# Attention products of two tensor-engine halves tied together, half 1 issued ahead of half 0

## The chip, the cores and the metric

The kernel runs on one core of a Trainium2 chip. Its engines work in parallel, each through its own queue and in that queue's order: TensorE (PE) multiplies matrices into PSUM banks, VectorE (DVE) and ScalarE (ACT) do the elementwise work and read PSUM, and SyncE (SP) issues the transfers from HBM. They wait for each other by semaphores. The metric is the time of one execution in microseconds (us), lower being better; a single core has one time per run.

## The reference

A first transformer block is followed by a network of two layers, over 256 tokens of width 1024, in float32. What matters here are its attention parts.

- The first block's mixer adds three things side by side: a gated linear attention (GLA, 4 heads), a causal convolution, and a differential attention with 4 heads, in which each head has two softmax maps over 64-wide halves of its queries and keys: `a = softmax(q1 k1^T) - lam * softmax(q2 k2^T)`, then `a v`. Group-routed experts follow.
- Each layer has a feed-forward block, a mixer and a second feed-forward block, all scaled by vectors that a large matrix `w_ada` gives from a condition `c` (`c_act @ w_ada`). The mixer adds a sparse attention with 8 heads (compressed, selected and window branches), a "forgetting" attention (FOX, 4 heads) whose scores get `F[q] - F[k]` added, and a block attention (MOBA, 4 heads). With 256 tokens, FOX and MOBA are plain causal softmax attentions with heads of width 64:

```
s = q k^T / 8   (+ F[q] - F[k] for FOX);  p = softmax(where(k <= q, s, -inf));  o = p v
```

## The kernel before

**Tiling.** Activations are kept with features on the 128 partitions. Weights come by DMA into `raw` tiles of 1 MB, ACT rounds them to a reduced float32 (`hi`, line 313), DVE computes the rest (`lo`, line 317), and PE multiplies with both. Most PE time is in these weight products (lines 334 to 355, 604, and the experts).

**Attention.** A head is 64 wide, half of PE's 128 rows or columns. In the scores (line 939 for the differential attention, line 1492 for FOX and MOBA in `causal`) the head of half 0 has its queries and keys on partitions 0 to 63, the head of half 1 on 64 to 127; each uses 64 of PE's rows. One set of scores has eight products: two halves, two heads `e`, and two query blocks, the first with 128 keys and the second with 256. The halves write different PSUM tiles: `pse` (half 0) and `psd` (half 1) in the differential attention, `psa` and `pse` in `causal`. Then come, on PE, the mask (`mask_pair`, lines 970 and 971; for FOX also the products with `NB`, line 1499), the row maxima on DVE (`neg_max`, 977 and 978), the exponentials on ACT (`act`, 487), scaling on DVE (957 and 958, or 1518 and 1519), transposes on PE (`prob_t`, 985 to 987, copied by 384 or 386), and the products with the values: 961 and 962 with full width, 1524 in `causal`, where each half uses 64 of PE's columns. These are in plain float32, and each such matmul is two records of the trace.

**The conditioning.** The products with `w_ada` (line 1060, tiles `araw` into `psm`) are spread over the whole program as a side job: `ada_step` takes one 1 MB tile, four matmuls that each use 32 of PE's columns (two per step in the last block of a layer). In the mixers the tiles come from a pool of two buffers, so the load of one waits until the matmuls of the one two before it are done.

**What sets the order.** The Python loops only give the dependencies and the program order. A list scheduler places the instructions of each engine by its own estimate of when each is ready; PSUM and SBUF pools with one or two buffers (rings `a`, `d`, `e` of two banks each, `n` and `m` of one) limit what is open. On the chip each engine then runs its list strictly in order. So in one engine's list the parts are mixed: weight products, conditioning and attention alternate. `after` (line 491) can add an ordering dependency without a semaphore between two instructions; before the change only the activation tables and the splits in `split` use it.

Of the kernel before, what the change touches and what calls it, by code (L numbers as in the profile page):

```python
# [20 lines left out]
P = 128  # L21
# [203 lines left out]
class Net:  # L225
# [266 lines left out]
    def after(self, ins, prev):  # L492
        self.tc.add_manual_dep(ins.ins, prev.ins.name, mybir.DependencyInfo(
            mybir.DependencyClass.NoSync, mybir.DependencyReason.DATA), reason="activation table")

    def table(self, name):
        ins = self.tc.keep_in_program_order(self.nc.scalar.preload_act_table_set(name))
        if self.tab is not None and self.tab[0] is self.nc.cur_bb:
            for p in [self.tab[1]] + self.tab[2]:
                self.after(ins, p)  # L500
        self.tab = (self.nc.cur_bb, ins, [])
# [308 lines left out]
    def gla(self, T, lr, gw, qk, gv, sog):  # L810


        nc = self.nc
        qT, kT = qk
# [5 lines left out]
        g = T([P, 256], "gg")  # L820
        self.log_sigmoid(g, L, 256, T)
        EX = T([P, 8, 256], "gEX")
        for t in range(2):
            for b in range(2):
                pe = self.ps("a")
                o = (t + 4 * b) * P
# [49 lines left out]
        for p in range(2):  # L876
            po = self.ps("a")

            for t, S_, o, q, st, sp in ((0, SA, 0, 0, True, True), (0, SX, 0, P, True, False), (1, SA, 4, P, False, True)):
                for e in range(2):  # L880
                    h = 2 * p + e
                    nc.tensor.matmul(po[64 * e:64 * e + 64, q:q + P], gv[:, t, 64 * h:64 * h + 64], S_[:, o + h, :], start=st,
                                     stop=sp, tile_position=(0, 64 * e))
            nc.scalar.activation(sq[:, 256 * p:256 * p + 256], po[:, 0:256], AF.Square)
            nc.vector.tensor_tensor(go[:, p, :], po[:, 0:256], sog[p], OP.mult)
        return go, sq

    def diff1(self, T, ss, nat, dv):
        nc = self.nc
# [5 lines left out]
        for i in range(2):  # L895
            for t in range(2):
                o = (2 * i + t) * 8
# [32 lines left out]
        for hp in range(2):  # L930
            pw = {}

            pms = [[self.ps(ring), self.ps(ring)] for ring in "ed"]
            for e in range(2):
                h = 2 * hp + e
                for i, (q, n) in enumerate(((0, P), (P, 256))):
                    for m in range(2):
                        r = slice(64 * m, 64 * m + 64)
                        nc.tensor.matmul(pms[m][i][:, e * n:e * n + n], qT[r, h, q:q + P], kT[r, h, 0:n], start=(e == 0),
                                         stop=False, skip_group_check=True)  # L940
            for m in range(2):
                p0, p1 = pms[m]
                self.mask_pair(p0, p1)
# [475 lines left out]
    def selected(self, T, kT, vn, qT, sg, po):  # L1419
# [3 lines left out]
        for rp in range(2):  # L1423
# [37 lines left out]
            for b in range(2):  # L1461
                for i in range(4):
                    for t, w in ((0, P0[i]), (1, P1[i])):
                        nc.vector.tensor_scalar(w[:, b], w[:, b], su[:, t, i // 2, i % 2, b:b + 1], None, OP.mult)

                for t, kt in ((0, 0), (1, 0), (1, 1)):
                    pt = self.ps("a")
                    for i in range(4):
                        src = P0[i][:, b] if t == 0 else P1[i][:, b, kt * P:(kt + 1) * P]
                        nc.tensor.transpose(pt[:, i * P:(i + 1) * P], src, ident)  # L1470
                    pT = T([P, 512], "apT", 3)
                    self.cp(pT, pt)
                    for g in range(2):
                        v0 = P * (1 + b) + 64 * g
                        nc.tensor.matmul(po[t][64 * g:64 * g + 64, 256 * rp:256 * rp + 256], vn[:, kt, v0:v0 + 64],  # L1475
                                         pT[:, 256 * g:256 * g + 256], start=False, stop=(b == 1 and kt == t and rp == 1),
                                         tile_position=(0, 64 * g), skip_group_check=True)

    def causal(self, T, mix, c0, qT, kT, ko, v, vo, NB):

# [3 lines left out]
        su = T([P, 4, 2], "su2", 2)  # L1484
        w0s = T([P, 2, 2, P], "aP0", 3)

        pms = [[self.ps(ring), self.ps(ring)] for ring in "ae"]
        for e in range(2):
            for i, (q, n) in enumerate(((0, P), (P, 256))):
                for hb in range(2):  # L1490
                    r = slice(64 * hb, 64 * hb + 64)
                    nc.tensor.matmul(pms[hb][i][:, e * n:e * n + n], qT[r, e, q:q + P], kT[r, ko + e, 0:n], start=(e == 0),
                                     stop=False, skip_group_check=True)
        for hb in range(2):
            p0, p1 = pms[hb]
            if NB is not None:
# [15 lines left out]
        for e in range(2):  # L1512
            po = self.ps("n")
            pTs = []
            for hb in range(2):
                h = 2 * e + hb
                w0, w1 = pw[h]
                nc.vector.tensor_scalar(w0, w0, su[:, h, 0:1], None, OP.mult)
                nc.vector.tensor_scalar(w1, w1, su[:, h, 1:2], None, OP.mult)
                pTs.append(self.prob_t(w0, w1))  # L1520
            for t in range(2):
                for hb in range(2):
                    o = vo + 64 * (2 * e + hb)
                    nc.tensor.matmul(po[64 * hb:64 * hb + 64, t * P:256], v[:, t, o:o + 64], pTs[hb][:, 256 * t:256 + P * t],
                                     start=(t == 0), stop=(t == 1), tile_position=(0, 64 * hb))
            self.put_hl(mix, c0 + e, po[:, 0:256])

    def final(self):
# [412 lines left out]
```

## Time and profile before

| | |
|---|---|
| Median of 3 runs | 1452.15 us (1451.53 to 1452.27) |
| Profiled execution | 1456.9 us, its span 1455.1 us |
| PE busy | 1411.1 us, 97% of the span |
| DVE busy | 1138.2 us, 78% |
| ACT busy | 856.0 us, 59% |
| HBM read | 324.13 MB, 223 GB/s over the span |

The places of the change are: the first mixer with line 939 (83 to 100 us) and the GLA products (116 to 118 us), the selected branch with line 1475 (from 633 us in layer 0, to 1207 us in layer 1), FOX and MOBA with lines 1492 and 1524 (671 to 699 us in layer 0, 1217 to 1243 us in layer 1). A matmul's busy time in the trace includes its way through the array, so that the records of consecutive matmuls overlap; what one costs is read from the start of the next.

### The profile page before, as it was taken

How to read it: one execution, taken by the hardware profiler on the slowest of the kernel's cores; microseconds unless marked ns; L12 is line 12 of the kernel's file. 1: busy time of each engine (PE TensorE's matmuls, PEld its weight loads, DVE VectorE, ACT ScalarE, POOL GpSimd, SP SyncE). 2: the span in 40 equal slices, each digit the busy share in tenths (PEclk: the TensorE clock that was granted, in tenths of full speed). 3: DMA queues.
4: the chain of work that ended last, by engine and by line, in shares of the span. 5: the costliest groups of instructions: out<-in, count | busy, mean ns of one | idle time of the engine just before them, and what ended most of it. 6: DMA issues, size and time to landing. Idle time of an engine off the chain costs nothing.

```text
span 1455.1 us, 22278 instructions
## 1 busy us (share of the span) xinstructions
PE 1411.1 (97%) x8093; PEld 1145.8 (79%) x8093; DVE 1138.2 (78%) x2557; ACT 856.0 (59%) x1575; POOL 0.2 (0%) x4
## 2 busy tenths in 40 slices
PE   7999699999999999999999999999999999999997
PEld 6755478778888888676788889888888677888886
DVE  8996478888999667485899886998687586887664
ACT  7545277777756555364755555666555464766553
POOL 0000000000000000000000000000000000000000
PEclk9999889999999999999999999999999999999999
DMA  8734557887887557543388686787477552275452
GB/s 306 276 129 165 236 202 261 298 324 275 326 318 271 198 184 266 194 169 116 136 294 309 226 297 214 284 315 261 159 263 290 211 194 87 90 241 191 158 179 69
DMA packets 51396, 326.67 MB, mean 224 GB/s; under 512 B 6209, under 2 KB 7378, under 8 KB 18898
## 3 DMA queue, kind: packets, MB, share of 16 engines
q1 hardware_dynamic: 50994, 325.00, 61.6%
q8 instruction: 65, 1.06, 0.3%
q14 instruction: 49, 0.40, 0.1%
q10 hardware_dynamic: 288, 0.20, 0.1%
HBM read 324.13 MB, written 1.05 MB: 223 GB/s over the span
## 4 chain that ended last, share of the span: by engine, by line
PE 79%; DVE 2%; ACT 2%; DMA 1%; issue 0%; DVEq 0%; ACTq 0%; SPq 0%
PE psd L337 12%; PE psa L337 11%; PE pse L337 10%; PE psd L339 7%; PE psa L339 6%; PE pse L339 5%; PE psd L353 2%; PE psm L1060 2%; PE psd L354 2%; PE psd L355 2%; PE psd L1732 1%; PE psd L1733 1%; PE psd L1731 1%; PE pse L1475 1%; PE pse L1754 1%; DVE lo L317 1%
## 5 line engine op out<-in xcount | busy, mean ns | idle before, releaser
L317 DVE TENSOR_TENSOR lo<-raw,hi 128x512 fp32r<-128x512 f32 x992 | 605.1, 639 | 164.9 <-ACT hi L313 162.6
L313 ACT ACTIVATE hi<-raw 128x1024 fp32r<-128x1024 f32 (+3 forms) x498 | 485.1, 980 | 347.7 <-PE psd L337 80.7
L337 PE MATMUL psd<-hl,hi 128*128 128x512 f32 x624 | 225.0, 402 | 7.8 <-ACT hi L313 7.0
L339 PE MATMUL psd<-hl,lo 128*128 128x256 f32 x656 | 185.0, 284 | 0.0
L337 PE MATMUL psa<-hl,hi 128*128 128x512 f32 x464 | 165.2, 397 | 1.2 <-ACT hi L313 1.2
L337 PE MATMUL pse<-hl,hi 128*128 128x512 f32 x464 | 164.3, 396 | 0.0
L337 PEld LDWEIGHTS psd<-hl,hi 128*128 128x128 f32 x624 | 117.9, 190 | 40.1 <-ACT hi L313 8.5
L339 PE MATMUL pse<-hl,lo 128*128 128x256 f32 x512 | 143.0, 280 | 0.0
L339 PE MATMUL psa<-hl,lo 128*128 128x256 f32 x496 | 138.7, 281 | 0.0
L339 PEld LDWEIGHTS psd<-hl,lo 128*128 128x128 f32 x656 | 124.7, 190 | 1.9 <-DVE lo L317 0.9
L337 PEld LDWEIGHTS psa<-hl,hi 128*128 128x128 f32 x464 | 87.2, 188 | 22.6 <-ACT hi L313 1.9
L337 PEld LDWEIGHTS pse<-hl,hi 128*128 128x128 f32 x464 | 87.3, 188 | 20.8 <-ACT w L384 0.3
L339 PEld LDWEIGHTS pse<-hl,lo 128*128 128x128 f32 x512 | 96.5, 189 | 0.2
L339 PEld LDWEIGHTS psa<-hl,lo 128*128 128x128 f32 x496 | 93.6, 189 | 0.8 <-DVE lo L317 0.4
L1089 DVE SCALAR_TENSOR_TENSOR acc<-araw,cact,acc 128x512 f32<-128x512 f32 x118 | 85.8, 748 | 1.6 <-DMA araw<-wada 1.6
L353 PE MATMUL psd<-hi,hl 128*128 128x512 f32 (+3 forms) x224 | 84.4, 377 | 0.8 <-ACT hl L375 0.4
L354 PE MATMUL psd<-lo,hl 128*128 128x512 f32 (+3 forms) x224 | 83.6, 373 | 0.0
L355 PE MATMUL psd<-hi,hl 128*128 128x512 f32 (+3 forms) x224 | 83.3, 374 | 0.0
L337 PE MATMUL psd<-hT,hi 128*128 128x512 f32 x220 | 77.6, 395 | 0.0
L337 PE MATMUL psa<-hT,hi 128*128 128x512 f32 x220 | 77.4, 394 | 0.0
L339 PE MATMUL psd<-hT,lo 128*128 128x256 f32 x264 | 74.2, 281 | 0.0
L339 PE MATMUL psa<-hT,lo 128*128 128x256 f32 x264 | 74.1, 281 | 0.0
(564 smaller groups left out, 2605.2 us busy)
## 6 DMA issues: line engine op xcount, KB each, us to landing
raw<-w SPq DMA_DIRECT2D x88, 1024.0 KB, 4.9
araw<-wada SPq DMA_DIRECT2D x64, 1024.0 KB, 6.7
raw<-w SPq DMA_DIRECT2D x64, 704.0 KB, 4.2
raw<-egu SPq DMA_DIRECT2D x32, 1024.0 KB, 5.0
raw<-edn SPq DMA_DIRECT2D x16, 1024.0 KB, 4.9
raw<-w2n SPq DMA_DIRECT2D x12, 1024.0 KB, 6.5
raw<-cw SPq DMA_DIRECT2D x8, 1024.0 KB, 5.8
araw<-wadb SPq DMA_DIRECT2D x8, 1024.0 KB, 5.7
```

The lines of the kernel that those rows point to most:

```text
L313: nc.scalar.activation(hi[:, f:g], src[:, f:g], AF.Copy)
L317: ins = nc.vector.tensor_tensor(lo[:, f:g], src[:, f:g], hi[:, f:g].bitcast(F32), OP.subtract)
L337: nc.tensor.matmul(ps[:M, :].rearrange("p (a b) -> p a b", a=2), hi[:, o:o + M], xhl[:, k0 + k, :, :], start=st, stop=False)
L339: nc.tensor.matmul(ps[:M, 0:256], lo[:, o:o + M], xhl[:, k0 + k, 0, :], start=False, stop=sp)
L353: nc.tensor.matmul(o, xh, wh, start=st, stop=False)
L354: nc.tensor.matmul(o, xh, wl, start=False, stop=False)
L355: nc.tensor.matmul(o, xl, wh, start=False, stop=sp)
L1060: self.nc.tensor.matmul(self.ada_acc[32 * j:32 * j + 32, :], lhsT, rhs[:, 512 * j:512 * j + 512], start=start, stop=stop, tile_position=(0 ...
L1089: nc.vector.scalar_tensor_tensor(acc[:, w], raw[:, w], self.cact[:, c, 0:1], acc[:, w], OP.mult, OP.add)
L1475: nc.tensor.matmul(po[t][64 * g:64 * g + 64, 256 * rp:256 * rp + 256], vn[:, kt, v0:v0 + 64], pT[:, 256 * g:256 * g + 256], start=False, s ...
L1731: nc.tensor.matmul(pg, xh(c), wh, start=(c == 0), stop=False)
L1732: nc.tensor.matmul(pg, xh(c), wl, start=False, stop=False)
```

## The change

A new helper `halves` issues the product of half 1, then that of half 0, and adds an ordering dependency between them, so that half 0 can't stand ahead of half 1 on PE. Where `prev` is given (the two score functions), the first product of a pair also follows the second product of the pair before, so that the eight products of a set keep one order. The dependency orders a pair; other instructions may still stand between. It is used in five places: GLA's values, the scores of the differential attention, the selected branch's values, and scores and values of `causal`. No product is added or removed.

```diff
--- before.py
+++ after.py
@@ -493,6 +493,15 @@
         self.tc.add_manual_dep(ins.ins, prev.ins.name, mybir.DependencyInfo(
             mybir.DependencyClass.NoSync, mybir.DependencyReason.DATA), reason="activation table")
 
+    def halves(self, product, prev=None):
+
+
+        first, second = (product(h) for h in (1, 0))
+        self.after(second, first)
+        if prev is not None:
+            self.after(first, prev)
+        return second
+
     def table(self, name):
         ins = self.tc.keep_in_program_order(self.nc.scalar.preload_act_table_set(name))
         if self.tab is not None and self.tab[0] is self.nc.cur_bb:
@@ -877,10 +886,9 @@
             po = self.ps("a")
 
             for t, S_, o, q, st, sp in ((0, SA, 0, 0, True, True), (0, SX, 0, P, True, False), (1, SA, 4, P, False, True)):
-                for e in range(2):
-                    h = 2 * p + e
-                    nc.tensor.matmul(po[64 * e:64 * e + 64, q:q + P], gv[:, t, 64 * h:64 * h + 64], S_[:, o + h, :], start=st,
-                                     stop=sp, tile_position=(0, 64 * e))
+                self.halves(lambda e: nc.tensor.matmul(
+                    po[64 * e:64 * e + 64, q:q + P], gv[:, t, 128 * p + 64 * e:128 * p + 64 * e + 64], S_[:, o + 2 * p + e, :],
+                    start=st, stop=sp, tile_position=(0, 64 * e)))
             nc.scalar.activation(sq[:, 256 * p:256 * p + 256], po[:, 0:256], AF.Square)
             nc.vector.tensor_tensor(go[:, p, :], po[:, 0:256], sog[p], OP.mult)
         return go, sq
@@ -930,14 +938,13 @@
         for hp in range(2):
             pw = {}
 
-            pms = [[self.ps(ring), self.ps(ring)] for ring in "ed"]
+            pms, pr = [[self.ps(ring), self.ps(ring)] for ring in "ed"], None
             for e in range(2):
                 h = 2 * hp + e
                 for i, (q, n) in enumerate(((0, P), (P, 256))):
-                    for m in range(2):
-                        r = slice(64 * m, 64 * m + 64)
-                        nc.tensor.matmul(pms[m][i][:, e * n:e * n + n], qT[r, h, q:q + P], kT[r, h, 0:n], start=(e == 0),
-                                         stop=False, skip_group_check=True)
+                    pr = self.halves(lambda m: nc.tensor.matmul(
+                        pms[m][i][:, e * n:e * n + n], qT[64 * m:64 * m + 64, h, q:q + P], kT[64 * m:64 * m + 64, h, 0:n],
+                        start=(e == 0), stop=False, skip_group_check=True), pr)
             for m in range(2):
                 p0, p1 = pms[m]
                 self.mask_pair(p0, p1)
@@ -1470,11 +1477,10 @@
                         nc.tensor.transpose(pt[:, i * P:(i + 1) * P], src, ident)
                     pT = T([P, 512], "apT", 3)
                     self.cp(pT, pt)
-                    for g in range(2):
-                        v0 = P * (1 + b) + 64 * g
-                        nc.tensor.matmul(po[t][64 * g:64 * g + 64, 256 * rp:256 * rp + 256], vn[:, kt, v0:v0 + 64],
-                                         pT[:, 256 * g:256 * g + 256], start=False, stop=(b == 1 and kt == t and rp == 1),
-                                         tile_position=(0, 64 * g), skip_group_check=True)
+                    self.halves(lambda g: nc.tensor.matmul(
+                        po[t][64 * g:64 * g + 64, 256 * rp:256 * rp + 256], vn[:, kt, P * (1 + b) + 64 * g:P * (1 + b) + 64 * g + 64],
+                        pT[:, 256 * g:256 * g + 256], start=False, stop=(b == 1 and kt == t and rp == 1),
+                        tile_position=(0, 64 * g), skip_group_check=True))
 
     def causal(self, T, mix, c0, qT, kT, ko, v, vo, NB):
 
@@ -1484,13 +1490,12 @@
         su = T([P, 4, 2], "su2", 2)
         w0s = T([P, 2, 2, P], "aP0", 3)
 
-        pms = [[self.ps(ring), self.ps(ring)] for ring in "ae"]
+        pms, pr = [[self.ps(ring), self.ps(ring)] for ring in "ae"], None
         for e in range(2):
             for i, (q, n) in enumerate(((0, P), (P, 256))):
-                for hb in range(2):
-                    r = slice(64 * hb, 64 * hb + 64)
-                    nc.tensor.matmul(pms[hb][i][:, e * n:e * n + n], qT[r, e, q:q + P], kT[r, ko + e, 0:n], start=(e == 0),
-                                     stop=False, skip_group_check=True)
+                pr = self.halves(lambda hb: nc.tensor.matmul(
+                    pms[hb][i][:, e * n:e * n + n], qT[64 * hb:64 * hb + 64, e, q:q + P], kT[64 * hb:64 * hb + 64, ko + e, 0:n],
+                    start=(e == 0), stop=False, skip_group_check=True), pr)
         for hb in range(2):
             p0, p1 = pms[hb]
             if NB is not None:
@@ -1519,10 +1524,9 @@
                 nc.vector.tensor_scalar(w1, w1, su[:, h, 1:2], None, OP.mult)
                 pTs.append(self.prob_t(w0, w1))
             for t in range(2):
-                for hb in range(2):
-                    o = vo + 64 * (2 * e + hb)
-                    nc.tensor.matmul(po[64 * hb:64 * hb + 64, t * P:256], v[:, t, o:o + 64], pTs[hb][:, 256 * t:256 + P * t],
-                                     start=(t == 0), stop=(t == 1), tile_position=(0, 64 * hb))
+                self.halves(lambda hb: nc.tensor.matmul(
+                    po[64 * hb:64 * hb + 64, t * P:256], v[:, t, vo + 64 * (2 * e + hb):vo + 64 * (2 * e + hb) + 64],
+                    pTs[hb][:, 256 * t:256 + P * t], start=(t == 0), stop=(t == 1), tile_position=(0, 64 * hb)))
             self.put_hl(mix, c0 + e, po[:, 0:256])
 
     def final(self):
```

The scheduler then places much else anew. On PE, in the first mixer (the second set of scores is `psd_938`, `psd_939` for half 1 and `pse_936`, `pse_937` for half 0; `araw_1253` to `araw_1271` are successive conditioning tiles; line 961 is line 968 after the change, 1060 is 1067), before:

```order
L1060 MATMUL psm_1248<-araw_1253,cact_363 32x512 x3
L1060 MATMUL psm_1248<-araw_1259,cact_363 32x512 x4
L863 MATMUL psa_1068<-hl_1040,gzk_1065 128x256 x2
L939 MATMUL psd_938<-dT_139_833,dT_136_818 128x128 x2
L970 LDWEIGHTS k_identb
L970 MATMUL psd_938<-k_maskb,k_identb 128x256
L939 MATMUL psd_939<-dT_139_833,dT_136_818 128x256 x2
L985 MATMUL pse_908<-blob,dP_158_880 128x128
L986 MATMUL pse_908<-blob,dP_159_881 128x128
L987 MATMUL pse_908<-blob,dP_159_881 128x128
```

and with the change, from the same place:

```order
L1067 MATMUL psm_1248<-araw_1259,cact_363 32x512 x3
L1067 MATMUL psm_1248<-araw_1265,cact_363 32x512 x4
L872 MATMUL psa_1068<-hl_1040,gzk_1065 128x256 x2
L945 MATMUL psd_938<-dT_139_833,dT_136_818 128x128
L992 MATMUL pse_908<-blob,dP_158_880 128x128
L993 MATMUL pse_908<-blob,dP_159_881 128x128
L994 MATMUL pse_908<-blob,dP_159_881 128x128
L1067 MATMUL psm_1248<-araw_1271,cact_363 32x512
L968 MATMUL pse_914<-w_169_912,ddv_795 128x256
L969 MATMUL pse_914<-w_169_912,ddv_795 128x128
```

Half 1 of the second set no longer runs ahead on its own (but for one product), and the conditioning stands one tile further on: `araw_1253` and one product of `araw_1259` have moved up into the first set of scores.

On PE, at the start of FOX in layer 0 (half 0 is `psa_7416`, `psa_7417`, half 1 is `pse_7418`, `pse_7419`; line 1492 is line 1496 after the change), before, from the first score product on:

```order
L1492 MATMUL psa_7416<-kd_6671 128x128
L1492 MATMUL psa_7417<-kd_6671 128x256
L1492 MATMUL psa_7416<-kd_6671 128x128
L1492 MATMUL psa_7417<-kd_6671 128x256
...
L1060 MATMUL psm_7637<-araw_7635,cact_363 32x512
L1492 MATMUL pse_7418<-kd_6671 128x128 x2
...
L1492 MATMUL pse_7419<-kd_6671 128x256 x2
```

and with the change, from the end of the weight products ahead of it:

```order
L1067 MATMUL psm_7637<-araw_7635,cact_363 32x512 x4
L1067 MATMUL psm_7637<-araw_7921,cact_363 32x512
L1496 MATMUL pse_7418<-kd_6671 128x128
L1496 MATMUL psa_7416<-kd_6671 128x128
L1067 MATMUL psm_7637<-araw_7921,cact_363 32x512 x2
L1496 MATMUL pse_7419<-kd_6671 128x256
L1496 MATMUL psa_7417<-kd_6671 128x256
L1496 MATMUL pse_7418<-kd_6671 128x128
L1496 MATMUL psa_7416<-kd_6671 128x128
L1496 MATMUL pse_7419<-kd_6671 128x256
L1496 MATMUL psa_7417<-kd_6671 128x256
```

The halves now alternate. Seven conditioning products (four of `araw_7635`, three of `araw_7921`) have moved ahead of the set or into it; the three of `araw_7921` stood before the change behind the output projection, where the next norm is computed.

## Rows read from the trace of the kernel before

**Rows 1.** The page: span, busy time of each engine, chain by engine.

```profile
span 1455.1 us, 22278 instructions
PE 1411.1 (97%) x8093; PEld 1145.8 (79%) x8093; DVE 1138.2 (78%) x2557; ACT 856.0 (59%) x1575; POOL 0.2 (0%) x4
PE 79%; DVE 2%; ACT 2%; DMA 1%; issue 0%; DVEq 0%; ACTq 0%; SPq 0%
```

**Rows 2.** Stretches: length, busy time (records) by engine, granted clock, DMA share.

```profile
100.00:110.00 10.00, 7.63 (x32) 3.03 (x31) 7.62 (x20) 2.12 (x9) 0.00 (x0) 0.84 0.55 212
671.00:680.00 9.00, 9.00 (x47) 4.82 (x48) 7.65 (x23) 6.24 (x21) 0.00 (x0) 1.00 0.33 117
1218.00:1230.00 12.00, 12.00 (x75) 8.00 (x74) 9.21 (x28) 6.51 (x22) 0.00 (x0) 1.00 0.25 87
```

**Rows 3.** Stretches, line 939 alone: length, PE, PEld, clock, DMA, GB/s.

```profile
82.00:86.00 4.00, 1.84 (x16) 1.41 (x16) 1.00 0.00 0
89.00:92.00 3.00, 1.84 (x8) 1.19 (x8) 1.00 0.83 339
96.00:100.00 4.00, 1.84 (x8) 1.19 (x8) 1.00 0.00 0
```

**Rows 4.** Stretches, line 1492 alone; the sum is over four sets.

```profile
670.00:677.00 7.00, 3.41 (x16) 2.30 (x16) 1.00 0.42 151
...
1225.00:1233.00 8.00, 3.93 (x16) 2.25 (x16) 1.00 0.00 0
sum 30.00, PE 14.26 PEld 8.77; mean PE 3.57 PEld 2.19
```

**Rows 5.** Stretches, line 1524 alone; the sum is over eight groups.

```profile
682.00:685.00 3.00, 1.51 (x8) 0.66 (x8) 1.00 0.61 251
686.00:688.00 2.00, 0.87 (x8) 0.49 (x8) 1.00 0.00 0
...
sum 17.00, PE 8.60 PEld 4.69; mean PE 1.07 PEld 0.59
```

**Rows 6.** DVE's waits from 75 to 130 us: total, times, longest.

```profile
DVE dqk L964 <- ACT w L963: 4.2, 2, 2.5
DVE mod L1104 <- PE psm L1100: 1.3, 1, 1.3
...
DVE w L386 <- PE pse L987: 0.9, 1, 0.9
```

**Rows 7.** PE in order of time: start, length, [idle time before, what ended it].

```profile
86.75 1.92 PE L1060 MATMUL psm<-araw,cact 128*32 128x512 f32 x14
...
92.76 0.70 PE L961 MATMUL pse<-w,ddv 128*128 128x256 f32 x2 [0.54 <-DVE w L386]
```

**Rows 8.** PE in order of time, later.

```profile
106.58 1.63 PE L1060 MATMUL psm<-araw,cact 128*32 128x512 f32 x2 [1.83 <-DMA araw<-wada]
108.14 1.22 PE L961 MATMUL pse<-w,ddv 128*128 128x256 f32 x2
```

**Rows 9.** SP's issues of the conditioning tiles: start; the first one's landing time.

```profile
87.86 0.33 SPq L1076 DMA_DIRECT2D araw<-wada  x1
DMA to landing us min/median/max: 4.8/4.8/4.8
```

**Rows 10.** The same, a later one.

```profile
101.55 0.33 SPq L1076 DMA_DIRECT2D araw<-wada  x1
```

**Rows 11.** Stretches, line 1060 alone, in layer 0: mixer, and next norm.

```profile
671.00:690.00 19.00, 3.14 (x8) 0.42 (x8) 1.00 0.32 112
712.00:721.00 9.00, 4.86 (x16) 0.88 (x16) 1.00 0.11 15
```

**Rows 12.** ACT in order of time: the normalized input of layer 0's second feed-forward.

```profile
720.55 1.72 ACT L375 ACTIVATE hl<-w,mod 128x256 fp32r<-128x256 f32 x4
```

**Rows 13.** PE in order of time: that input's first product.

```profile
726.75 0.39 PE L337 MATMUL psd<-hl,hi 128*128 128x512 f32 x1
```

**Rows 14.** ACT in order of time: the conditioning's row copy in the first mixer.

```profile
120.28 0.60 ACT L1097 ACTIVATE adarow<-psm 128x512 f32<-128x512 f32 x1 [2.23 <-PE psm L1060]
```

## The prediction

> **What bounds the kernel now.** The page comes first. PE is busy for 1411.1 of 1455.1 us, and of the chain that ended last it holds 79%, DVE and ACT 2% each and DMA 1% [rows 1]. So PE is the limit over the whole, and DVE with its 78% mostly keeps out of the way. That is an average, so I next read the stretches in which the change works [rows 2]. The reader is to look at PE's second figure against the stretch's length. From 671 to 680 us (FOX of layer 0) PE is busy for 9.00 of 9.00 us, from 1218 to 1230 (FOX and the start of MOBA in layer 1) for 12.00 of 12.00: PE work taken away there is time taken away, as long as what follows doesn't wait. From 100 to 110 us (the first mixer) PE has 7.63 of 10, DVE 7.62 of 10, and the granted clock is 0.84: nobody is full there, the engines wait for each other, and PE work taken away is worth nothing by itself. The two kinds of places need two kinds of sums.
>
> **FOX and MOBA, scores.** What the two halves are worth side by side can be read from before, because the first set of line 939 had them alternating and the second did not [rows 3]. Alternating, 16 records (eight products, both halves) take 1.84 us. In the second set the eight records of one half take 1.84 us alone, and those of the other half 1.84 again, 7 us later. So a product runs beside its neighbour of the other half for nothing, and a pair that is torn costs 1.84 / 8 = 0.23 per product. In line 1492 before, the halves are apart in each of four sets, which take 14.26 us together [rows 4]. Four alternating sets take 4 x 1.84 = 7.36. Gain 6.90 us.
>
> **FOX and MOBA, values.** Line 1524 has eight groups of eight records. Where the halves stood next to each other a group took 0.87 us, where transposes stood between them 1.51, and all eight take 8.60 [rows 5]. With the change 8 x 0.87 = 6.96, gain 1.64. The loads of weights show the same: 0.49 us for eight in the one group, 0.66 in the other. The two halves here use the same rows of PE and differ in columns only. The Trainium skill, page "TensorE: Matmul & The Clock Gate", section "Part 3: Packing small matmuls", says that a weight load overlaps running matmuls only when its row group differs; by that these pairs would gain nothing, and the sum would be 1.64 less. The trace speaks against it here, with 0.87 beside 1.51, so I keep the term.
>
> **What the layers give back.** First, torn pairs: the new order still has conditioning products inside a set. One torn pair for each of four sets at 0.23 is 0.92. Second, in layer 1 two transposes of a conditioning row now stand inside the FOX scores, and these need ACT's copy of that row, which took 0.60 in the first mixer [rows 14]; PE would wait for it once: 0.60. Third, the norm transitions. In layer 0, three conditioning products that filled PE behind the output projection have moved ahead. That filler was 4.86 us for 16 records (eight products), while in the mixer eight records took 3.14 us [rows 11]; a product there is 4.86 / 8 = 0.61, three are 1.8. If this cover goes, PE may stand still for up to 1.8 us in each of two layers (3.6). It costs nothing if other work still covers: the normalized input is ready from 720.55 us [rows 12] and PE first uses it at 726.75 [rows 13], so 6.2 us of work lie between. I take 0.5 per layer, nearer to nothing, 1.0. The conditioning itself costs the same wherever it stands, the count of its products being unchanged. Layers: 6.90 + 1.64 - 0.92 - 0.60 - 1.0 = 6.0 us.
>
> GLA's values and the selected branch are edited too. What pairs torn there could be worth is bounded by one group of line 1524, 1.51 - 0.87 = 0.64 us [rows 5], and their products already stand in pairs; torn anew they lose as much. I take zero.
>
> **The first mixer.** Before, DVE's three largest waits from 75 to 130 us sum to 4.2 + 1.3 + 0.9 = 6.4 us [rows 6]; the largest ended on the softmax pieces of line 963, which hang on PE. Why PE was late is seen in its list. Seven conditioning products stand at 86.75 us, and the first output product at 92.76 [rows 7]. The load of the next tile is issued at 87.86, when a buffer came free [rows 9], but the one after that only at 101.55 [rows 10], and lands 4.8 us later, at 106.35. PE, in order, stood before it at 106.58 after 1.83 us of waiting, and then ran the next output product in 1.22 us instead of 0.70, the granted clock having fallen [rows 7, 8]. Behind those products are queued the transposes and output products for which DVE waited.
>
> With the change the conditioning stands one tile further on. `araw_1253`, done at about 87.7 before, is done within the first set of scores, by about 84.6, so the next load, `araw_1265`, is issued there and lands at about 84.6 + 4.8 = 89.4. Its four products follow three others behind 86.75, so PE is there at about 88 to 89 and waits near 1 us. `araw_1271` follows the release of `araw_1259` at about 89 and lands at about 93.8; PE's next stop on it is ahead of the output product that ran at 92.76, so about 1 us again is added to it. SP's queue holds nothing else that these pass. Queued behind PE's stops are the score products of half 1 and the output products, and DVE waits for those. Also, half 1 of the second set is no longer 7 us early: its softmax starts later by about the 2 us that its scores and masks take, since both halves come as one. For DVE I sum about 1.0 (output product), 1.6 (the late half) and 0.5 (the second maxima), 3.1 after against 6.4 before: 3.3 gained. The half clock goes with the 106.58 stop: 1.22 - 0.70 = 0.5. Together 3.8. Bounds: 6.4 gained if every wait goes; below, the loss of the slow rival.
>
> **Sum.** 6.0 + 3.8 = 9.8; 1456.9 - 9.8 = 1447.1 for the profiled execution. That one was 4.75 above the median of the runs, 1452.15, so the median comes to 1442.35: 1442.
>
> **Rivals.** First: the first mixer gives nothing. For it: 100 to 110 us has neither engine full, so the chain through softmax may be the limit whatever PE does. Against: that stretch contains a DMA wait with nothing but order behind it [rows 8]. Time 1452.15 - 6.0 = 1446.2.
>
> Second: the layers' gain is given back. PE reaches the next norm 6 us earlier over two layers, but the softmax chain through DVE and ACT, busy for 7.65 and 6.24 of 9 us [rows 2], may set when that norm can start, so that PE just waits there. Against: PE is full through the mixer and DVE is not. Only the mixer's 3.8 stays: 1448.3.
>
> Third, the slow one: the tiles arrive late every time. Conditioning moved forward demands four landings (1265, 1271, 1283, 1289) sooner, and in-order PE stops before each with the softmax queued behind. Price: DVE's 4.2 us of waits [rows 6] hung on one such stop before; four make 16.8, 12.6 more. Against the layers' 6.0: 1452.15 + 6.6 = 1458.8. From the third stop on it decides (8.4 more against 6.0, 1454.6); with two (4.2 more) the layers still win. For it: a landing takes 4.8 us and there are two buffers. Against: the buffers come free earlier by the same move.
>
> That the change doesn't do what it says: other work may stand between a pair. The list on PE shows pairs next to each other nearly throughout, so I give this no case of its own beyond the torn pairs.
>
> **Chances.** Forecast 0.55, first rival 0.20, second 0.14, third 0.11. 0.2% is 2.9 us, about what a measurement of this kernel can tell from no change. Faster by more: the forecast, the first rival and half of the second (3.8 is near 2.9), 0.55 + 0.20 + 0.07 = 0.82; within: the other half and 0.01 of the third, 0.08; slower 0.10. The likeliest case's own range is 1438 to 1446: with 6.4 in the mixer and nothing for the transitions it is 1452.15 - 7.0 - 6.4 = 1438.7, with nothing in the mixer 1446.2. The range reaches on to the second rival and a little past it, 1449.5, and down to 1436: 6.4 in the mixer and all 8.5 of the pairs is 1437.2, less about 1 if an odd conditioning product runs beside the halves.
>
> **What would show it.** Right: line 1496 (the scores) at about 1.84 us for each set and line 1527 (the values) at 0.87 for each group, PE still full through FOX and MOBA; in 85 to 115 us at most two waits for a conditioning tile, of about 1 us, and clock 1.00 where it was 0.84; the block's output projection starting about 4 us earlier. PE gaps ahead of the second feed-forward, or a wait of about 0.6 for the row copy inside layer 1's FOX, show those terms. Wrong: sets that stay near 3.5 although the halves alternate (then the overlap isn't the alternation's), a mixer with three or more stops, or PE gaps of 3 us at each norm (then DVE's chain bounds).

## The result and the profile after

The changed kernel took 1442.85 us (median of 6 runs, 1441.24 to 1447.02) against 1452.21 us for the kernel before in the same rounds (6 runs, 1451.53 to 1453.57): ratio 0.9932, 95% interval 0.9919 to 0.9945, 9.4 us faster. The forecast was 1442 us, faster. The total came out right; the working below it did so only in parts.

The page of the changed kernel, its first rows, for [rows 1]:

```profile
span 1441.4 us, 22271 instructions
PE 1396.4 (97%) x8089; PEld 1139.9 (79%) x8093; DVE 1137.5 (79%) x2557; ACT 855.7 (59%) x1575; POOL 0.2 (0%) x4
```

PE is busy for 14.7 us less, and still for 97% of the span. That is more than the pairs can give, so other things shrank too. The scores of FOX and MOBA in the changed kernel (line 1496, four sets; for [rows 4]):

```profile
662.00:668.00 6.00, 1.85 (x16) 1.21 (x16) 1.00 0.91 330
676.00:682.00 6.00, 1.85 (x16) 1.21 (x16) 1.00 1.00 356
1206.00:1211.00 5.00, 2.08 (x16) 1.47 (x16) 1.00 0.45 185
1217.00:1222.00 5.00, 1.85 (x16) 1.21 (x16) 1.00 0.28 90
sum 22.00, PE 7.63 PEld 5.11; mean PE 1.91 PEld 1.28
```

And their values (line 1527, the first two of eight groups, and the sum; for [rows 5]):

```profile
674.50:677.00 2.50, 0.87 (x8) 0.49 (x8) 1.00 0.78 288
677.00:680.00 3.00, 0.87 (x8) 0.49 (x8) 1.00 1.01 391
...
sum 20.50, PE 6.97 PEld 3.88; mean PE 0.87 PEld 0.48
```

Both fell close to what was forecast (7.36 and 6.96): 14.26 to 7.63 us and 8.60 to 6.97. Three of the four sets stand at 1.85 us, the third at 2.08. The first mixer of the changed kernel: the stretch from 100 to 110 us (for [rows 2]), DVE's waits (for [rows 6]), and PE where it meets the tile `araw_1265` (for [rows 8]).

```profile
100.00:110.00 10.00, 9.66 (x55) 5.76 (x54) 9.81 (x26) 3.36 (x17) 0.00 (x0) 1.00 0.46 156
```

```profile
DVE dqk L971 <- ACT w L970: 1.8, 2, 1.3
DVE hl L785 <- ACT hl L784: 1.3, 2, 1.1
DVE gzk L863 <- PE psa L872: 1.2, 1, 1.2
```

```profile
89.50 0.64 PE L1067 MATMUL psm<-araw,cact 128*32 128x512 f32 x4 [0.46 <-DMA araw<-wada]
```

PE now has 9.66 of 10 us there and DVE 9.81, where both had 7.6. The wait for the tile is 0.46 us and ends at 89.50 (89.4 was worked out); no other wait for a tile is left in the mixer. PE's longest waits there are now 1.2 us ahead of a conditioning product (117.88 us) and 1.0 us on DVE (92.99 us).

**Where the time went, stretch by stretch.** For each instruction of DVE and ACT that can be matched in two traces, I took the start after minus the start before, and the median of it in each stretch. Where the engines run the same list the shift is constant to 0.1 us, so its steps show where time was gained. Negative is earlier. In us against the first profile of the kernel before; the last column is the mean granted clock from 84 to 125 us:

```
run            mixer  routing  to L0 mixer  L0 mixer   L0 FOX to    to L1   L1 FOX   clock
               1      of MoE                start      end of FFN   mixer   to end   84-125
before, again  -1.71  -0.66    -0.19        +0.03      +0.06        +0.03   +0.11    1.00
changed        -4.70  -3.99    -0.69        -0.05      -3.41        +0.02   -1.04    1.00
changed, again -2.96  -2.69    -0.68        +0.11      -3.30        -0.02   -1.04    0.96
e1_diff        -4.59  -2.64    -0.65        +0.15      +0.04        +0.03   +0.16    1.00
e4_causal      -0.21  -2.95    +0.95        -1.58      -3.41        +0.01   -1.17    0.96
e2_scores      -0.13  -0.30    +0.77        -1.36      -4.66        +1.69   -0.76    0.96
e3_values      -0.02  -2.46    +0.33        -1.61      -1.50        +1.73   +0.28    0.96
e6_noprev      -0.08  -2.84    +0.15        -1.66      -6.14        +0.00   -1.24    0.96
e7_zero_first  -2.84  -2.93    -0.20        -1.49      -3.81        +1.63   -0.20    0.96
e9_cover       -4.70  -2.71    -0.62        +0.01      -5.05        +1.71   +0.32    1.00
e11_cover0     -4.68  -4.03    -0.72        -1.43      -3.69        +1.59   -1.12    1.00
e10_early      -0.96  -3.06    +0.06        -1.60      +0.05        +0.01   +0.13    0.96
e12_late       -0.43  -2.62    -0.02        -1.66      +0.05        -0.03   +0.13    0.96
```

Three columns belong to the change: the first mixer, layer 0 and layer 1. The others move in kernels that don't differ there, e3_values and e10_early among them: the routing by up to 4.0 us, the starts of the two layers' mixers by up to 1.7 each, all three at stretches of half clock that come and go, and the stretch up to layer 0's mixer by up to 1.0, at full clock in every profile. A kernel's median holds a mixture of them.

### The profile page after: what moved, and what is told of

It reads as the page before. It is cut to its first block, busy times and chain, and to the rows that moved or that the text cites. A ratio compares the mean times of both kernels' runs of the same rounds, so it can differ in the third digit from the quotient of the medians.

```text
span 1441.4 us, 22271 instructions
## 1 busy us (share of the span) xinstructions
PE 1396.4 (97%) x8089; PEld 1139.9 (79%) x8093; DVE 1137.5 (79%) x2557; ACT 855.7 (59%) x1575; POOL 0.2 (0%) x4
## 4 chain that ended last, share of the span: by engine, by line
PE 80%; DVE 2%; ACT 1%; issue 0%; DMA 0%; DVEq 0%; ACTq 0%
PE psd L337 12%; PE psa L337 11%; PE pse L337 10%; PE psd L339 7%; PE psa L339 6%; PE pse L339 6%; PE psd L353 2%; PE psm L1067 2%; PE psd L354 2%; PE psd L355 2%; PE psd L1736 1%; PE psd L1737 1%; PE psd L1735 1%; PE pse L1758 1%; PE pse L1760 1%; PE pse L1759 1%
```

## The experiments

Twelve runs were made: ten more kernels, and a second profile of each of the two. Ratios are to the kernel before on the same chip; where the medians blur, the table decides.

**e1_diff: the first mixer alone.**

```diff
     # kernel before, plus `halves`, used in diff1 only
+    pr = self.halves(lambda m: nc.tensor.matmul(pms[m][i][:, e * n:e * n + n], ...), pr)
```

> Only the scores of the differential attention (first mixer) have their halves tied; everything else as in the kernel before. Theory (the first mixer's waits are a part of their own): DVE's waits on the softmax pieces fall from 4.2 to about 2 us, no wait for a conditioning tile above 1 us, the output projection starts about 4.6 us earlier as in the changed kernel, and the layers' sets stay at 14.26 us: 1447.6 us. Rival (the mixer is bound by its softmax chain whatever PE does, the whole gain is in the layers): 1452 us. Rival (the mixer carries it all, the layers give all back): 1443 us.

Measured 1449.04 us, ratio 0.9963 (0.9950 to 0.9976). The mixer stands at -4.59 as in the changed kernel (both at clock 1.00, where the first profile of before has 0.96; see e8_before), DVE's wait on the softmax pieces at 1.8 us, the layers at +0.04 and +0.16. The first theory holds: the mixer gains by itself.

**e4_causal: FOX and MOBA alone.**

```diff
     # kernel before, plus `halves`, used in causal only (scores and values)
+    pr = self.halves(lambda hb: nc.tensor.matmul(pms[hb][i][:, e * n:e * n + n], ...), pr)
+    self.halves(lambda hb: nc.tensor.matmul(po[64 * hb:64 * hb + 64, t * P:256], ...))
```

> Only FOX and MOBA (scores and values) have their halves tied; first mixer, GLA and selected branch as before. Theory: scores give 6.2 us and values 1.5, of which about 3.3 are given back at the two norm transitions (PE gaps of 1.5 us in layer 0 and 2.1 in layer 1, a half-clock stretch of some 3 us after the first): 1447.8 us, and with the mixer's own run the two parts add up to the whole change, so that GLA and the selected branch are worth nothing. Rival (nothing given back): 1444.5 us. Rival (all given back, the norm chain bounds): 1452 us.

Measured 1447.91 us, ratio 0.9965 (0.9953 to 0.9978). Layer 0 at -3.41 and layer 1 at -1.17, as in the changed kernel (-3.41, -1.04): 4.6 us of 7.7 arrive. With e1_diff the columns add up to the whole change, so GLA and the selected branch show no worth of their own beside 0.1 us.

**e2_scores and e3_values: one kind of product alone.**

```diff
     # e2_scores: halves in the scores of causal only; e3_values: in its values only
```

> Only the scores of FOX and MOBA are tied; the conditioning of the second feed-forward moves into FOX and MOBA as in the changed kernel. Theory: the four sets fall to about 1.85 us each (6.2 us saved), the norm transitions lose their cover and give about 3.3 us back, so 2.9 us net in the two layers (stretch by stretch against the kernel before: layer 0 about -2.3, layer 1 about -0.6), near 1449.5 us. Rival (the give-back comes with the values): -6 in the layers, no gaps ahead of the second feed-forward, 1446.

Measured 1448.48 us, ratio 0.9962 (0.9947 to 0.9977); layers -4.66 and -0.76, 5.4 together, not 2.9. Here the expectation missed. In layer 0 PE again waited 0.9 us ahead of the second feed-forward (1.48 us with both kinds tied), but the clock stayed at 1.00, where it falls with both kinds tied (below). The half-clock stretch is worth 1.65 of the 2.5.

> Only the values of FOX and MOBA are tied; the conditioning keeps its place behind the norm's sum of squares. Theory: every group of eight takes 0.87 us (from 8.60 to 6.97 in all), nothing is given back, -1.5 us in the layers, near 1451 us, no gap and clock 1.00 ahead of the second feed-forward. Rival (pairs that differ only in columns gain nothing): 0.0 us in the layers. Rival (any tie loses the cover): +1 to +2 us.

Measured 1453.39 us, ratio 1.0005 (0.9996 to 1.0015), no change. By the table the layers gained 1.50 and lost 0.28, as the first theory has it, and in the profiled execution a half-clock stretch at the start of layer 1's mixer (+1.73) took it back. That the same happened in the runs that make up the median is not shown. The rival that pairs differing only in columns gain nothing falls: PE came out of the layers earlier.

**e8_before: the kernel before, a second profile.** No edit.

> The kernel before, unchanged, for a second profile. Theory (the 4.7 us by which the first profiled execution lay above the median of its runs are a longer stretch at half clock behind the routing of the experts, 180 to 200 us, that varies from run to run): a span near 1450.5 us, the granted clock 1.00 again from about 185 us, all other stretches within 0.2 us of the first profile. Rival (the whole execution was slower, or profiling adds it): the same 0.66 to 0.73 clock at 180 to 200 us, span near 1455.

Measured 1455.27 us in that one run. The theory was wrong in its place: the routing was slow again. From 165 to 205 us in the first profile of before, in the second, and in the changed kernel:

```profile
165.00:185.00 20.00, 10.07 (x39) 5.80 (x40) 9.86 (x58) 6.63 (x10) 0.00 (x0) 0.58 0.66 267
185.00:205.00 20.00, 20.00 (x88) 16.70 (x87) 10.51 (x20) 12.79 (x18) 0.00 (x0) 0.82 0.44 154
```

```profile
165.00:185.00 20.00, 11.58 (x45) 7.09 (x46) 10.40 (x51) 7.96 (x11) 0.00 (x0) 0.57 0.66 252
185.00:205.00 20.00, 20.00 (x89) 16.75 (x88) 10.62 (x19) 12.60 (x17) 0.00 (x0) 0.83 0.48 172
```

```profile
165.00:185.00 20.00, 13.31 (x53) 9.43 (x45) 9.96 (x24) 11.44 (x18) 0.00 (x0) 0.64 0.69 262
185.00:205.00 20.00, 19.90 (x99) 16.38 (x99) 14.92 (x27) 15.10 (x19) 0.00 (x0) 1.00 0.66 244
```

It was in the mixer that the second profile differed. From 84 to 125 us, in the first profile of before, and in the second:

```profile
84.00:125.00 41.00, 36.68 (x194) 18.24 (x191) 33.43 (x84) 14.39 (x54) 0.00 (x0) 0.96 0.48 180
```

```profile
84.00:125.00 41.00, 36.81 (x201) 18.83 (x202) 35.14 (x88) 16.05 (x59) 0.00 (x0) 1.00 0.49 180
```

The same list ran 1.71 us faster with the clock at 1.00; 0.04 x 41 us is 1.64. So the mixer's gain has to be read at equal clock.

**e13_after: the changed kernel, a second profile.** No edit.

> The changed kernel again, for a second profile and for its time on the same chip as the three others. Theory: first mixer -3.0 to -4.7 against the kernel before (whose own two profiles differ there by 1.7), layer 0 at -3.4, layer 1 at -1.0, both within 0.1 us of the first profile, since nothing in them changes from run to run; what differs lies behind the routing (170 to 205 us) and at the starts of the layers' mixers (600, 1160 us), with a clock below 1.00. Rival (the layers' share is itself chance): more than 0.5 us off there.

Measured 1444.17 us, ratio 0.9935 (0.9918 to 0.9952). Layer 0 at -3.30 and layer 1 at -1.04 repeat the first profile; the theory holds. The mixer, 84 to 125 us, had the half clock this time:

```profile
84.00:125.00 41.00, 37.63 (x200) 18.80 (x203) 35.72 (x89) 17.59 (x61) 0.00 (x0) 0.96 0.52 180
```

At clock 1.00 the mixer is 4.70 - 1.71 = 3.0 us faster than before, at 0.96 it is 2.96: the change is worth 3.0 us there either way. (DVE's wait on the softmax pieces was 3.4 us in this profile, 1.8 in the first.)

**e10_early and e12_late: is it the tile or the order of the halves?**

```diff
     # e10_early: kernel before, nothing tied
+        self.ada(2)                                   # ahead of the loop in diff1
+                        if hp == 0 and e == 1:
+                            self.after(ins, self.ada_last)
     # e12_late: diff1 tied, conditioning ordered back (tile and column group -> what it follows)
+        self.late = {(1, 1): s[0], (1, 2): s[0], (1, 3): s[0], (3, 0): o[0], (3, 1): s[1], (3, 2): s[1], (3, 3): s[1]}
```

> The kernel before with no halves tied; in the first mixer two conditioning tiles are called ahead of the differential attention, and the second half of its first set of scores is ordered behind them, so that the conditioning stands one tile further on while the halves of the second set stay apart, 7 us from each other. Theory (the mixer's gain comes from the tiles being loaded earlier): no wait of 1.8 us for a conditioning tile, clock 1.00 at 105 to 110 us, DVE's wait on the softmax pieces at 1 to 2 us, the output projection starts 3 to 4.7 us earlier, 1448 us. Rival (it comes from the halves standing together): the output projection within 1 us of the kernel before, 1452. Rival in between (both): -1.5 to -2.5.

Measured 1452.12 us, ratio 0.9996 (0.9985 to 1.0008). The mixer gained 0.96 us at clock 0.96. The wait for the tile is gone, as PE's waits from 84 to 125 us show; PE now waits for the copies of the softmax pieces instead:

```profile
PE pse L964 <- DVE w L386: 2.0, 2, 1.3
PE psm L1103 <- ACT adarow L1100: 0.7, 1, 0.7
```

The output projection started 1.3 us earlier, not 3 to 4.7. My first theory falls: calling the tiles early does not bring the mixer's gain by itself. The edit also holds back the second half of the first set of scores, and what that cost is not separated.

> Only the differential attention is tied (as in the run that did this alone, which started the output projection 4.6 us earlier), and the conditioning in the first mixer is ordered back to where the kernel before has it: the second and third tile behind the first set of scores, the fourth behind the first output product and the second set. Theory after the run with early conditioning and untied halves (it gained only 1 us of the 4.6): the order of the halves carries the mixer, and the tile's place little; the output projection 3 to 4 us earlier than before. Rival (both are needed, the stop before the fourth tile takes it back): a wait of about 1.8 us for the tile near 106 us and 1.5 us or less earlier.

Measured 1450.60 us, ratio 0.9983 (0.9973 to 0.9994). PE's waits from 84 to 125 us:

```profile
PE psa L805 <- DVE cy L803: 1.5, 1, 1.5
PE psm L1076 <- DMA araw<-wada: 1.1, 1, 1.1
```

The output projection started at 124.97 us (129.79 before, 125.26 in the changed kernel), earlier still than the theory said. But then PE stood for 1.29 us and ran 16 records of the conditioning that had been put off:

```profile
129.35 0.50 PE L337 MATMUL psd<-hl,hi 128*128 128x512 f32 x1 [1.29 <-DVE hl L789]
...
131.76 1.92 PE L1076 MATMUL psm<-araw,cact 128*32 128x512 f32 x16
```

Of 4.3 us only 0.43 were left from 150 us on, where the shift is constant. So the theory fell and the rival held, though PE's wait for the tile was 1.1 us, at 120 us. All at equal clock: the tiles moved early alone gave 1.0, the order of the halves alone 0.4, and both 3.0: the order brings the attention forward, and the conditioning must be out of the way for that to last.

**e6_noprev: pairs without the chain.**

```diff
-        if prev is not None:
-            self.after(first, prev)
```

> The changed kernel without the chain from pair to pair: each pair is ordered, the eight products of a set are not. On PE the first mixer then comes out in the order of the kernel before (half 1 of the second set alone, 7 us ahead), FOX and MOBA still in pairs. Theory: first mixer 0 us, layers -4 to -5 as in the changed kernel, near 1447.5. Rival (the pair alone is what counts, in the mixer too): 1443.

Measured 1445.28 us, ratio 0.9954 (0.9940 to 0.9969). The mixer gained nothing (-0.08): there the chain is the change. The layers gained 7.4 us, 3 more than with it and more than the 4 to 5 expected. PE waited 0.7 us in layer 0 behind MOBA instead of 1.48, with the clock at 1.00, which is 0.8 + 1.65 of the 3.

**e7_zero_first: half 0 first.**

```diff
-        first, second = (product(h) for h in (1, 0))
+        first, second = (product(h) for h in (0, 1))
```

> The changed kernel with half 0 issued ahead of half 1 in every pair. The conditioning in the first mixer keeps the place that it has in the changed kernel, and in layer 0 three of its products stand behind MOBA again. Theory (what counts is that the halves stand together; which goes first does not): sets at 1.85 us, mixer -3 to -4.7, layers between -4.4 and -5.5, 1442 to 1443. Rival (the late half must go first, or PE stops at its tile with the other half done): waits on PE ahead of the sets, 1 us or more each of four, 1447.

Measured 1445.25 us, ratio 0.9941 (0.9921 to 0.9961). Mixer -2.84 at clock 0.96 (the changed kernel has -2.96 there), layer 0 -3.81, layer 1 -0.20. The half that goes first hardly matters; standing together does. Layer 1 lost 0.8 us, which I did not follow up.

**e9_cover and e11_cover0: the cover given back.**

```diff
         r = self.rstd(self.nps[:, :256], 1.0 / D)
+        self.ada_behind = self.sqm if f else None      # e11_cover0: ... if f and l == 0 else None
         self.ada(n0)                                   # ada_mm: self.after(ins, self.ada_behind)
+        self.ada_behind = None
```

> The changed kernel, with the conditioning of each layer's second feed-forward (two tiles in layer 0, one in layer 1) ordered on PE behind the first product of the norm's sum of squares, where it stood before the change. Theory (the transition's lost cover gave back about 3.3 us): no PE gaps ahead of the second feed-forward, clock 1.00 there, 1439.5 us against the changed kernel's 1442.9. Rival (the norm chain on DVE and ACT sets the start, cover or not): 1442.9. Rival (the conditioning that moved forward fills PE inside FOX and MOBA, and PE would wait there without it): gaps there instead, 1443 to 1446.

Measured 1444.42 us, ratio 0.9944 (0.9926 to 0.9962). The changed kernel ahead of the second feed-forward of layer 0: PE's waits from 700 to 725 us, and 707 to 722.

```profile
PE psd L339 <- DVE lo L317: 0.8, 1, 0.8
PE psm L1107 <- ACT adarow L1104: 0.7, 1, 0.7
```

```profile
707.00:722.00 15.00, 13.52 (x70) 10.06 (x70) 14.85 (x35) 10.55 (x19) 0.00 (x0) 0.89 0.25 81
```

The same place in e9_cover, 705 to 720:

```profile
705.00:720.00 15.00, 15.00 (x85) 10.32 (x85) 13.88 (x34) 10.60 (x19) 0.00 (x0) 1.00 0.62 215
```

With the cover PE has no gap and the clock stays up; layer 0 gains 5.05 instead of 3.41. In the changed kernel 1.48 us of PE standing still were followed by a stretch at half clock, 0.11 x 15 = 1.65 us. The first gap ended with ACT's copy of a conditioning row, the second with a weight tile of DVE, which was busy for 14.85 of 15 us. In layer 1 the rival held: PE waited 1.9 us in FOX where the conditioning had been, and the layer came out at +0.32.

> The changed kernel with the conditioning ordered behind the norm's sum of squares in layer 0 alone; in layer 1, where the run with both held lost 3.1 us against the changed kernel (PE waited 1.6 us in FOX for the input that the conditioning had covered), it stays where the change puts it. Theory (cover is needed where the gap is: in layer 0 behind the norm, in layer 1 inside FOX): layer 0 at -5.0 us instead of -3.5 against the kernel before, layer 1 at -1.0 as in the changed kernel; 1.6 us under the changed kernel, 1441.3. Rival (what layer 0 gains comes back as a wait in layer 1 or behind the second feed-forward): 1442.9.

Measured 1442.90 us, ratio 0.9930 (0.9917 to 0.9944), the same as the changed kernel. (Of the 3.1 us put on layer 1 in that text, 1.7 lie ahead of its FOX, at a half-clock stretch; 1.4 are its own.) Layer 1 came back to -1.12. Layer 0 up to 735 us followed e9_cover, and then its second feed-forward ran slower through: by 815 us it had lost 1.4 against it, on the same list. What that was is below. Up to that feed-forward, at 735 us, PE's starts in layer 0 had gained 3.5 us in both kernels with the cover, and 1.8 in the changed kernel at 747 (times of the kernel before): the gain of the cover is real in its place and not shown in the total.

No version here beats the changed kernel clearly. e6_noprev's layers with the chain kept in the first mixer alone would be the one to try; it was not run.

## Why the prediction was right, point by point

**Right:** that PE is the limit in FOX and MOBA, that a pair costs one product where it stands together, and both sizes. By the starts of PE's records (each start to the next, in layers 0 and 1, waits left out) line 1492 went from 13.24 to 6.96 us, a gain of 6.28 against 6.90 - 0.92 = 5.98; the values from 7.90 to 6.41, 1.49 against 1.64. The Trainium skill, "TensorE: Matmul & The Clock Gate", "Part 3: Packing small matmuls", has a rule that a weight load overlaps running matmuls only when its row group differs, from which the prediction took a rival of zero for the second (the same section also lists a speedup of 2.38x for three products packed by columns). 0.87 us in all eight groups decide against that rule for these products, which differ in columns. Right too: the conditioning tile's landing, the count of waits for it, the start of the output projection (4.5 us earlier, of which 1.7 is the half clock that only the first profile of before had there), and zero for GLA and the selected branch.

Two slips in it did no harm. Eight products are four pairs, so by [rows 3] a torn pair costs 1.84 / 4 = 0.46 on average, not 0.23, and the term for four would have been 1.84; but in the changed kernel only one pair is torn, by the row transposes in layer 1's FOX, and its set took 0.23 more than the others. And DVE's third largest wait before was 1.0 us (`DVE hl L776 <- ACT hl L775: 1.0, 1, 1.0`), not the 0.9 of [rows 6].

**Mis-sized: the norm transitions.** The step "I take 0.5 per layer, nearer to nothing" failed. The slack of 6.2 us between the normalized input and its first use [rows 12, 13] consisted of products (line 604, now 613) that ran earlier once the filler was gone, while the norm was computed. In the changed kernel 1.2 us of it were left:

```profile
711.43 1.71 ACT L375 ACTIVATE hl<-w,mod 128x256 fp32r<-128x256 f32 x4
712.64 0.43 PE L337 MATMUL psd<-hl,hi 128*128 128x512 f32 x1
```

Then PE stood for 0.68 us until ACT's row copy, a wait that the prediction had only in layer 1, and 0.80 us until DVE's weight tile. DVE had been as full in that window before (14.66 of 15 us) without a wait of PE. Layer 0 lost 1.48 us of gaps and 1.65 of half clock. PE's waits in layer 1, 1195 to 1285 us:

```profile
PE pse L337 <- DVE w L619: 0.7, 1, 0.7
PE pse L992 <- DVE aP L1523: 0.5, 1, 0.5
PE pse L337 <- ACT hl L375: 0.3, 1, 0.3
PE pse L1496 <- DVE w L386: 0.3, 1, 0.3
PE psm L1107 <- ACT adarow L1104: 0.3, 1, 0.3
```

The two of line 337 are at the transition: 1.48 + 1.65 + 0.7 + 0.3 = 4.1 against 1.0. The wait for the row copy inside layer 1's FOX was 0.3 us instead of 0.60, beside two others in FOX and MOBA of 0.3 and 0.5. So the second rival was true for the larger part in size: of 7.8 us of pairs 5.2 were given back, the sum of these gaps, waits and the half clock.

**Partly luck:** the layers still gained 3.4 + 1.0 = 4.4 us (forecast 6.0), where 7.8 - 5.2 is 2.6. From 747 to 830 us the second feed-forward of layer 0 ran 1.6 us faster on an unchanged list, which no term had. This does not close the account: by the starts of PE's records, the weight products of lines 334 to 339 took 1.35 us less in layer 0 (670 to 830 us before) and 1.3 more in layer 1 (1195 to 1300 us); the rest are pieces under 0.8 us that were not followed. Line 337 and 339 before, and after:

```profile
762.43 0.40 PE L337 MATMUL psd<-hl,hi 128*128 128x512 f32 x1
762.66 0.28 PE L339 MATMUL psd<-hl,lo 128*128 128x256 f32 x1
762.77 0.40 PE L337 MATMUL psd<-hl,hi 128*128 128x512 f32 x1
```

```profile
751.28 0.39 PE L337 MATMUL psd<-hl,hi 128*128 128x512 f32 x1
751.51 0.28 PE L339 MATMUL psd<-hl,lo 128*128 128x256 f32 x1
751.63 0.39 PE L337 MATMUL psd<-hl,hi 128*128 128x512 f32 x1
```

The mean distance of such pairs from 740 to 800 us is 353 ns before and 347 after, both at granted clock 1.00.

**The first mixer:** 3.8 forecast, 3.0 measured at equal clock. The 0.5 for the half clock was no part of the change: that stretch comes and goes with either list. The 3.3 for DVE's waits stands against these 3.0, which is close, but my cause, the late tile, carries a third of it alone (1.0, e10_early); the order of the halves alone carries 0.4, and more than half needs both.

**The total:** 3.0 + 3.4 + 1.0 = 7.4 us are placed, of 9.8 forecast. The median moved by 9.4 (interval 8.0 to 11.8). The other 2.0 are not placed. Less half clock in the changed kernel's runs does not explain them: the granted clock was 0.990 in the mean of its 12 timed runs and 0.991 in 53 of the kernel before, and among the runs at 0.991 the mean span was 1440.2 us (5 runs) against 1450.9 (18 runs). So the forecast of 1442 was met with the help of 2 us that no term had; that part is luck.

## What to carry to other kernels

Here products on different halves of the array cost no more side by side than one alone (sets of 16 records in 1.85 us against 3.4 to 3.9), so keep them adjacent in issue order, and count a saved PE microsecond only up to the next place where another engine must deliver. Before taking filler out from behind a reduction or norm, look what PE will wait for there: the price is the gap and then, in some kernels, the clock. With runs of such size, match instruction starts between two traces stretch by stretch; the total of a kernel hides gains of 1 to 3 us under stretches at half clock.

## What the runs showed of the hardware that was not expected

Half-clock stretches of 1.6 to 1.7 us of loss appear or not, on the same list, at several places where PE had just stood idle, for 0.5 to 2.4 us in all. At the start of layer 1's mixer in e9_cover, and in the changed kernel, with the same PE list:

```profile
1138.00:1148.00 10.00, 8.54 (x83) 4.85 (x85) 4.07 (x14) 3.27 (x15) 0.00 (x0) 0.83 0.85 325
```

```profile
1139.00:1149.00 10.00, 8.64 (x90) 4.69 (x93) 4.84 (x17) 4.98 (x19) 0.00 (x0) 1.00 0.92 365
```

PE is busy for nearly the same share in both; 0.17 x 10 us is the loss.

A steady stretch of weight products has two paces, 353 and 347 ns per pair of lines 337 and 339, at granted clock 1.00. The kernels before, e1_diff, e3_values, e10_early, e12_late and e11_cover0 ran layer 0's second feed-forward at 353, the changed kernel, e2_scores, e4_causal, e6_noprev, e7_zero_first and e9_cover at 347, although e9_cover and e11_cover0 have the same list there. Of the seven kernels that tie the scores of FOX and MOBA all but e11_cover0 ran at 347, and of those that don't, none did. What sets it was not found.
